# A bound on outstanding row gathers, and half of a projection in plain fp32

## The chip, the cores and the metric

The kernel runs on one core of a Trainium2 chip. The metric is the device time of one execution in microseconds (us). The core has five engines that run side by side and wait for each other through semaphores: PE (TensorE, matmuls; its weight loads are told apart as PEld), DVE (VectorE), ACT (ScalarE), POOL (GpSimd) and SP (SyncE, which here only issues DMAs). Each engine works off its own queue strictly in order.

## The reference

A decoder layer for one sequence of 256 tokens, model width 2048. First a mixer: one input projection to 4096 columns, whose first half feeds a gated linear recurrence (8 tiles of 128 channels) and whose second half feeds a gated causal convolution with 31 taps (8 tiles), and an output projection. Then a retrieval layer:

```python
proj = h @ w_in                                     # 256 x 2048 @ 2048 x 4096
lru_x, lru_g, conf_v, conf_g = jnp.split(proj, 4 parts of 1024)
...
z = causal_depthwise_conv(conf_v * sigmoid(conf_g), conf_dw_w, conf_dw_b)
y = jnp.concatenate([y_lru, silu(layer_norm(z))]) @ w_out
...
q = (h @ wq).reshape(t, 8 heads, 2, 128)
scores = einsum('thpd,hpnd->thpn', q, subkeys)      # 2 x 128 scores a head
...                                                 # top 16 of each half, top 16 of their sums
u = jnp.take(u_table, expert_idx, axis=0)           # 16384 x 2048, 128 rows a token
act = jnp.einsum('cd,chkd->chk', h, u)
v = jnp.take(v_table, expert_idx, axis=0)
out = jnp.einsum('chk,chkd->cd', gates * gelu(act), v)
```

## The kernel before

Activations lie transposed, 128 channels on the partitions and 256 tokens beside each other. A matrix in fp32 is split into a part h that PE takes in its faster fp32 form (fp32r in the rows) and a remainder l: ACT copies (line 94), DVE subtracts (line 95). A product is then three matmuls: h by h, h by l, l by h (lines 351, 352, 354 in `slab`).

**The projection** (about 40 to 345 us). Ten of the 32 column tiles are begun early (`begin`), while the modulation vectors are made; the other 22 go through `proj`, each as two slabs of 8 row blocks of 128. A slab takes a buffer of the ring `fring` for its loaded weights and one each of `Hring` and `Lring` for the split. `conf` and `lru` call `proj` and put their own work on DVE, the 31 taps of the convolution above all (line 422). `modstep` puts a piece of other modulation matrices (line 276) between slabs. A scheduler orders the instructions of each engine by priorities. When the last convolution is summed (line 426), `confln` normalises (lines 473 and 476), and the output projection follows.

**The score stage** (about 496 to 1235 us). For eight heads the queries are made, and then the scores of all 128 x 128 experts' first 1536 columns are multiplied densely, a row of 128 experts at a time (`upiece`, `piece`: lines 762, 765, 766, 768), in 304 pieces of weights (256 of `u`, 48 of `wq`). The remaining 512 columns of the 128 experts of each token are fetched: a unit is one expert rank of 128 tokens, a gather (line 704, an indirect DMA issued by POOL) brings 128 rows of 2 KB into a buffer, and a dot product on DVE (line 710) uses it. There are 256 units; a head's end makes 32 new ones. The order on DVE is written by hand: after each piece `fill` spends what time DVE has left over, on the top-k of the heads (`tops`) or on dot products. `gathers` issues gathers as long as there are a free buffer, a unit and credit of transfer time:

```python
while free and units and clock[2] > 0:
    g = free.pop(0)
...
elif dots and dots[0][3] + LAG <= clock[0]:
    clock[1] -= dot()
```

`clock[0]` counts pieces, and a dot product comes at least `LAG` = 3 pieces behind its gather. The buffers are 6 in the region R and 30 in S, where rows of the score matrix come to stand later (`lend`, `retire`). A gather into a buffer that has been used before waits for the dot product that read it.

Of the kernel before, what the change touches and what calls it, by code (L numbers as in the profile page):

```python
# [21 lines left out]
T = 256  # L22
D = 2048
KT = D // 128
# [9 lines left out]
HP = 120  # L34
# [4 lines left out]
DOTS = 3  # L39
SLACK = 0  # L40
UG = 2
BURST = 1
AHEAD = 10
RB = 8
# [42 lines left out]
def build(nc, tc, A, stop=None):  # L87
# [5 lines left out]
    def split(h, l, src, eng=None):  # L93
        nc.scalar.activation(h, src, AF.Copy)  # L94
        (eng or nc.vector).tensor_tensor(l, src, h, op=OP.subtract)  # L95
# [65 lines left out]
    class Ring:  # L161
# [4 lines left out]
        def __call__(self):  # L166
# [8 lines left out]
    hH = lambda k: hcol(0, k)  # L175
    hL = lambda k: hcol(1, k)
# [6 lines left out]
    fring = PF.ring(4, KT // 2, 128)  # L183
    Hring = Ring([PR.t(8, 128) for i in range(3)] + [sb.t(8, 128)])
    Lring = Ring([PR.t(8, 128) for i in range(2)] + [sb.t(8, 128) for i in range(2)])
    yH, yL = PR.t(KT, T), PR.t(KT, T)
    xT = PF.t(KT, T)
    xn = yT = PF.t(KT, T)
    zc = yT[:, CT:, :]

    spare = [[v[:, a:a + 4, :].rearrange("p a b -> p (a b)").rearrange("p (k c) -> p k c", c=128) for a in at]
             for v, at in ((yT, (4,)), (yH, (8, 12)), (yL, (8, 12)))]
    zrow = PF.t(512, dt=BF)[:1]
    nc.gpsimd.memset(zrow, 0.0)
    ar = Area(0, RKB)
# [13 lines left out]
    xpR = tr_(2, T + LK - 1)  # L209
    zR = tr_(3, T + CK - 1)  # L210
    mx = ar.t(T)

    psA = ExitStack()
    pp = psA.enter_context(pool("pp", NPP, space=PSUM))
# [49 lines left out]
    def modfull(m, new, misc, ring, st, n, dma, k0=0, k1=KT):  # L264


        ps = new()
        for a in range(0, D, n):
            for k in range(k0, k1):
                t = ring()  # L270
                with tc.high_priority(offset=HP):
                    dma.dma_start(t.rearrange("p (g c) -> p g c", g=4),
                                  wm[k * 128:(k + 1) * 128, m * D:m * D + D]
                                  .rearrange("p (g c) -> p g c", g=4)[:, :, a // 4:(a + n) // 4])
                for g in range(4):
                    nc.tensor.matmul(ps[32 * g:32 * g + 32, a // 4:(a + n) // 4], cs32[:, k, :],  # L276
                                     t[:, g * n // 4:(g + 1) * n // 4], start=k == k0, stop=k == k1 - 1,
                                     tile_position=(0, 32 * g))
                if k < k1 - 1 or a + n < D:
                    yield  # L280
        s = st()
        nc.scalar.activation(s, ps, AF.Copy)
        tp = misc()
        for q in range(4):
            nc.tensor.transpose(tp[:, 128 * q:128 * q + 128], s[:, 128 * q:128 * q + 128], ident)
        nc.vector.tensor_tensor(pick(modc[:, m, :]), tp.rearrange("p (q j r) -> p j q r", q=4, r=32)[:, :, :, 0],
                                pick(bmc[:, m * KT:m * KT + KT] if k0 == 0 else modc[:, m, :]), op=OP.add)
        yield
# [46 lines left out]
    def hchunk(j):  # L335
        sl = slice(4 * j, 4 * j + 4)
        nc.vector.scalar_tensor_tensor(a1[:, sl], modc[:, 1, sl], 1.0, col("g_pre_mix")[:, sl], op0=OP.add, op1=OP.mult)
        for k in range(4 * j, 4 * j + 4):
            nc.vector.tensor_scalar(xn[:, k, :], xn[:, k, :], a1[:, k:k + 1], modc[:, 0, k:k + 1], op0=OP.mult, op1=OP.add)
            split(hH(k), hL(k), xn[:, k, :])  # L340

    KH = KT // 2

    def slab(ps, src, k0, k1, rh, rl, first, last):
        n = k1 - k0
        w, h, l = (x()[:, :n, :] for x in (fring, Hring, Lring))
        with tc.high_priority(offset=HP):
            nc.sync.dma_start(w, src[:, k0:k1, :])
            split(h, l, w)
        for k in range(k0, k1):  # L350
            nc.tensor.matmul(ps, h[:, k - k0, :], rh(k), start=first and k == k0, stop=False)  # L351
            nc.tensor.matmul(ps, h[:, k - k0, :], rl(k), start=False, stop=False)  # L352
        for k in range(k0, k1):
            nc.tensor.matmul(ps, l[:, k - k0, :], rh(k), start=False, stop=last and k == k1 - 1)  # L354

    mring = lambda: wring().rearrange("p a b -> p (a b)")
    mods = itertools.chain(*(modfull(m, lambda: pp.tile([128, 512], F32, name="modps"), misc, mring, modsR, D, nc.sync)
                             for m in (2, 4, 3)))

    def modstep(n=1):  # L360
        for _ in range(n):
            next(mods, None)
# [14 lines left out]
    for j in range(4):  # L377
# [5 lines left out]
                        begin(j - 1, i)  # L383
                n += 1
        hchunk(j)
    rings = fring, Hring, Lring
    for r, more in zip(rings, spare):
        r.aps = r.aps + more
    for i in range(NFIRST):
# [5 lines left out]
    def proj(ct):  # L395
        if ct in begun:
            i = ct // CT % 2
            return begun.pop(ct)[:, (1 - i if ct >= 2 * CT else i) * T:][:, :T]
        ps = accum()
        for a in range(2):  # L400
            slab(ps, A["w_in"][ct], a * KH, a * KH + KH, hH, hL, a == 0, a == 1)
            modstep(next(mcount))
        return ps

    zs = yT[:, 0, :]
    lwa = PCOLS["lru_conv_w"][0]

    def conf(c):
        pg = proj(3 * CT + c)
        sg = sgR()  # L410
        nc.scalar.activation(sg, pg, AF.Tanh, scale=0.5)
        pv = proj(2 * CT + c)
        z = zR()
        nc.gpsimd.memset(z[:, :CK - 1], 0.0)
        nc.vector.scalar_tensor_tensor(z[:, CK - 1:], sg, 1.0, pv, op0=OP.add, op1=OP.mult)
        o = zc[:, c, :]
        for j in range(CK):
            wcol = wdw[:, j * CT + c:j * CT + c + 1]
            if j == 0:
                nc.vector.tensor_scalar(o, z[:, 0:T], wcol, col("conf_dw_b", c), op0=OP.mult, op1=OP.add)  # L420
            else:
                nc.vector.scalar_tensor_tensor(o, z[:, j:j + T], wcol, o, op0=OP.mult, op1=OP.add)  # L422
        if c == 1:
            nc.vector.tensor_tensor(zs, zc[:, 0, :], o, op=OP.add)
        elif c:
            nc.vector.tensor_tensor(zs, zs, o, op=OP.add)

    def lru(c):
        px = proj(c)
        lw = lwR().rearrange("p (a b) -> p a b", a=2)  # L430
        nc.sync.dma_start(lw, A["wax"][c])
# [71 lines left out]
    last = []  # L503
    GO = 4
    for g in range(0, KT, GO):
# [6 lines left out]
        for i in range(GO):  # L512
            k = g + i
# [5 lines left out]
            if k == KT - 1:  # L519
                last = to  # L520
# [85 lines left out]
    def flat(a, n):  # L606

        return Sf[:, a * T:(a + n) * T]
# [24 lines left out]
    units = []  # L633
# [62 lines left out]
    tops, free, dots, gone, lent, late = [], list(guS), [], [], {}, []  # L696
    clock = [0, 0.0, 0.0]

    def gathers():
        while free and units and clock[2] > 0:  # L700
            clock[2] -= GU * 512 / 360
            g = free.pop(0)
            tt, s_ = units.pop(0)
            nc.gpsimd.indirect_dma_start(out=g, out_offset=None, in_=A["ug"],  # L704
                                         in_offset=bass.IndirectOffsetOnAxis(ap=ei[:, tt, s_:s_ + 1], axis=0))
            dots.append((g, tt, s_, clock[0]))

    def dot():
        g, tt, s_, _ = dots.pop(0)
        nc.vector.scalar_tensor_tensor(gjR(), g, 1.0, h2n[:, tt, :GU], op0=OP.mult, op1=OP.mult,  # L710
                                       accum_out=actg[:, tt, s_:s_ + 1])
        if not any(g is x for x in gone):
            free.append(g)
        return dve(GU)

    def retire(r):
# [11 lines left out]
    def lend(at):  # L728
        lent[at] = flat(at, UG)[:, :GU]
        free.append(lent[at])  # L730

    def fill(ns, load, pe):

        clock[0] += 1
        clock[1] += ns
        clock[2] = min(clock[2] + (pe - load) * DMAF, BURST * GU * 512 / 360)
        gathers()
# [53 lines left out]

    for at in list(range(12, 60 - 3 * XUF - UG, UG)) + list(range(102, 129 - UG, UG)):
        lend(at)
    more = [flat(60 - 3 * i - 3, 3) for i in range(XUF)]
    with tc.manual_schedule(engines={mybir.EngineType.DVE}):
        for h in range(NH):
# [15 lines left out]
            for tt in range(2):  # L812
                ps = misc()
# [21 lines left out]
    last = xa.ring(int(xa.end - xa.at) // (UW * 128), UW * 128).aps  # L835
    with tc.manual_schedule(engines={mybir.EngineType.DVE}):
        while urows or state["parts"]:
            upiece()
        while dots or units:
            clock[2] = 1e9  # L840
            gathers()
            dot()
# [6 lines left out]
    for tt in range(2):  # L849
        ps = misc()  # L850
# [99 lines left out]
    for tt in range(2):  # L950
# [7 lines left out]
        ps = pm.tile([128, 512], F32, name="pm")  # L958
# [6 lines left out]
    ps = pm.tile([128, 512], F32, name="pm")  # L965
# [10 lines left out]
    units = [(tt, s_) for tt in range(2) for s_ in range(NK)]  # L976
# [34 lines left out]
    def vload(r, eng=None):  # L1011
        v, vh, vl = vfR(), vHr(), vLr()
        with tc.high_priority(offset=HPV):
            nc.sync.dma_start(v, A["vd"][r])
            split(vh, vl, v, eng)
        return vh, vl
# [17 lines left out]
    with tc.manual_schedule(engines=MANV):  # L1034
# [3 lines left out]
        for r in range(NK):  # L1038
            if r < 2:
                vmul(r, ws[r], vs[r], (1,))  # L1040
            else:
                v, w = vload(r), wnext
# [28 lines left out]
    with tc.manual_schedule(engines=MANV):  # L1071
        for tt in range(2):
# [10 lines left out]
            for n in (3, 0, 1, 2):  # L1083
                c = slice(512 * n, 512 * n + 512)
                src = out[tt][n] if c.stop <= DV else og[:, tt, :]
# [48 lines left out]
```

## Time and profile before

| what | value |
|---|---|
| runs | 2002.36 us median of 3 (2001.26 to 2014.05) |
| the profiled execution | 1990.23 us, its span 1988.5 us |
| busy share of the span | PE 92%, PEld 79%, DVE 77%, ACT 49%, POOL 34% |
| bytes moved by DMA | 530.07 MB, mean 267 GB/s |
| largest shares of the chain that ended last | PE 55%, issue 16%, POOL 11%, DMA 9%, DVE 5% |

The profile is of one execution. Times in its rows are counted from the start of the span. "Busy" is the time in which an engine had an instruction under way; matmuls overlap, so that one of them lasts longer than the time from its start to the next one's. The granted clock is 1.00 at PE's upper level (2.4 GHz) and 0.50 at its lower (1.2 GHz). "issue" as the end of a wait means that the profile names nothing that was waited for.

### The profile page before, as it was taken

To read this page: it belongs to the slowest core of one execution; us is meant where nothing else is said; L and a number is where in the kernel's file an instruction comes from. 1 tells how busy PE (TensorE), PEld (TensorE's weight loads), DVE (VectorE), ACT (ScalarE), POOL (GpSimd) and SP (SyncE) were. 2 spreads that over 40 slices of the span, in tenths; PEclk is the share of its full clock that TensorE was granted. 3 is DMA by queue.
4 is the path that set the end of the run, shared out by engine and by line. 5 is a ranking of instruction groups with operands and counts; after the bars stand their busy time and mean duration, and the time that the engine had idled before them with its cause. 6 is when DMAs were issued, how large, how long until landed. Compare 5 with 4: busy or idle time off the path is not lost.

```text
span 1988.5 us, 34804 instructions
## 1 busy us (share of the span) xinstructions
PE 1827.9 (92%) x12408; PEld 1580.1 (79%) x12408; DVE 1530.5 (77%) x3834; ACT 972.3 (49%) x1512; POOL 674.8 (34%) x577
## 2 busy tenths in 40 slices
PE   7897999898949699999899999999999999999996
PEld 3675787685949699999899999789877777778874
DVE  3249999755729489999787775789788888888887
ACT  3244434743625355555455555567544444544453
POOL 0000000000061432323543442224377666666662
PEclk8999999998979799999999999999999999999998
DMA  9988868686776677778898887742499898888884
GB/s 326 373 313 320 281 229 317 262 287 245 230 239 195 216 252 256 261 244 280 289 300 274 290 289 221 212 139 81 131 319 329 327 324 310 313 300 316 311 303 161
DMA packets 174799, 530.07 MB, mean 267 GB/s; under 512 B 20753, under 2 KB 44449, under 8 KB 167201
## 3 DMA queue, kind: packets, MB, share of 16 engines
q1 hardware_dynamic: 132656, 391.50, 57.8%
q0 software_dynamic: 40960, 134.25, 20.0%
q8 instruction: 97, 1.59, 0.3%
q10 hardware_dynamic: 1008, 2.10, 0.3%
q14 instruction: 78, 0.63, 0.1%
HBM read 521.40 MB, written 6.37 MB: 265 GB/s over the span
## 4 chain that ended last, share of the span: by engine, by line
PE 55%; issue 16%; POOL 11%; DMA 9%; DVE 5%; ACT 2%; another core or an unknown queue 1%; POOLq 0%; SPq 0%; ACTq 0%; DVEq 0%
PE acc L765 11%; PE acc L766 11%; PE acc L768 11%; POOL S L996 7%; PE acc L354 4%; PE acc L351 4%; PE acc L352 3%; PE W L945 3%; PE modps L276 3%; PE G L920 2%; DMA PF<-in_w_mod_dram 2%; POOL sl L996 2%; DMA PF<-in_w_in_dram 2%; POOL sh L996 2%; DVE PF L422 2%
## 5 line engine op out<-in xcount | busy, mean ns | idle before, releaser
L765 PE MATMUL acc<-sh,sb 128*128 128x256 f32 x1792 | 453.4, 288 | 36.8 <-issue 23.2
L766 PE MATMUL acc<-sl,sb 128*128 128x256 f32 x1792 | 452.1, 287 | 0.3 <-issue 0.3
L765 PEld LDWEIGHTS acc<-sh,sb 128*128 128x128 f32 x1792 | 349.3, 195 | 42.0 <-issue 25.1
L766 PEld LDWEIGHTS acc<-sl,sb 128*128 128x128 f32 x1792 | 349.3, 195 | 2.3 <-issue 2.2
L94 ACT ACTIVATE sb<-R 128x768 fp32r<-128x768 f32 (+2 forms) x203 | 196.8, 970 | 262.3 <-PE acc L766 115.2
L95 DVE TENSOR_TENSOR sb<-S,sb 128x768 fp32r<-128x768 f32 (+3 forms) x272 | 219.8, 809 | 130.7 <-ACT sb L94 106.1
L768 PE MATMUL acc<-sh,sb 128*128 128x256 f32 x1792 | 269.3, 285 | 9.9 <-issue 9.3
L94 ACT ACTIVATE sb<-S 128x768 fp32r<-128x768 f32 (+3 forms) x274 | 207.4, 759 | 140.0 <-PE acc L766 85.9
L996 POOL DMA_INDIRECT S<-in_vg_dram,ei x158 | 212.7, 1346 | 112.3 <-DVE R L1005 82.5
L768 PEld LDWEIGHTS acc<-sh,sb 128*128 128x128 f32 x1792 | 240.0, 194 | 10.1 <-issue 9.1
L704 POOL DMA_INDIRECT R<-in_ug_dram,ei x111 | 112.5, 1013 | 390.7 <-DMA R<-in_ud_dram 252.3
L95 DVE TENSOR_TENSOR sb<-R,sb 128x768 fp32r<-128x768 f32 (+1 forms) x160 | 150.2, 939 | 109.7 <-ACT sb L94 64.7
L704 POOL DMA_INDIRECT S<-in_ug_dram,ei x145 | 147.0, 1014 | 246.8 <-DVE R L710 156.3
L1023 PE MATMUL o<-sl,sb 128*128 128x512 f32 x900 | 221.4, 394 | 9.9 <-DVE sl L95 8.2
L1023 PE MATMUL o<-sh,sb 128*128 128x512 f32 x888 | 219.0, 395 | 10.1 <-DVE sh L95 9.3
L1023 PEld LDWEIGHTS o<-sl,sb 128*128 128x128 f32 x900 | 166.6, 188 | 53.8 <-DVE sl L95 17.9
L1023 PEld LDWEIGHTS o<-sh,sb 128*128 128x128 f32 x888 | 165.8, 189 | 53.9 <-DVE sh L95 18.2
L94 ACT ACTIVATE PR<-PF 128x1024 fp32r<-128x1024 f32 (+2 forms) x99 | 85.0, 868 | 127.5 <-DMA PF<-in_w_in_dram 85.5
L1023 PE MATMUL o<-sb 128*128 128x512 f32 x516 | 126.8, 391 | 1.5 <-ACT sb L94 1.5
L1005 DVE SCALAR_TENSOR_TENSOR R<-S,R 128x512 f32<-128x512 f32 x157 | 117.3, 747 | 3.5 <-DMA S<-in_vg_dram,ei 0.7
L351 PE MATMUL acc<-sh,PR 128*128 128x256 f32 x412 | 107.4, 296 | 8.8 <-ACT PR L94 7.1
L1023 PEld LDWEIGHTS o<-sb 128*128 128x128 f32 x516 | 96.6, 188 | 23.2 <-ACT sb L94 2.8
(304 smaller groups left out, 3436.3 us busy)
## 6 DMA issues: line engine op xcount, KB each, us to landing
R<-in_vd_dram SPq DMA_DIRECT2D x128, 768.0 KB
PF<-in_w_mod_dram SPq DMA_DIRECT2D x86, 1024.0 KB
R<-in_ud_dram SPq DMA_DIRECT2D x132, 384.0 KB
S<-in_ud_dram SPq DMA_DIRECT2D x124, 384.0 KB
PF<-in_w_in_dram SPq DMA_DIRECT2D x44, 512.0 KB
PF<-in_w_out_dram SPq DMA_DIRECT2D x32, 512.0 KB
PF<-in_w_in_dram SPq DMA_DIRECT2D x40, 256.0 KB
sl<-in_w_mod_dram SPq DMA_DIRECT2D x20, 512.0 KB
```

What stands on the lines that cost most here:

```text
L94: nc.scalar.activation(h, src, AF.Copy)
L95: (eng or nc.vector).tensor_tensor(l, src, h, op=OP.subtract)
L276: nc.tensor.matmul(ps[32 * g:32 * g + 32, a // 4:(a + n) // 4], cs32[:, k, :], t[:, g * n // 4:(g + 1) * n // 4], start=k == k0, stop=k == ...
L351: nc.tensor.matmul(ps, h[:, k - k0, :], rh(k), start=first and k == k0, stop=False)
L354: nc.tensor.matmul(ps, l[:, k - k0, :], rh(k), start=False, stop=last and k == k1 - 1)
L704: nc.gpsimd.indirect_dma_start(out=g, out_offset=None, in_=A["ug"], in_offset=bass.IndirectOffsetOnAxis(ap=ei[:, tt, s_:s_ + 1], axis=0))
L765: nc.tensor.matmul(ps, uh[:, k - k0, :], hH(k), start=k == 0, stop=False)
L766: nc.tensor.matmul(ps, uh[:, k - k0, :], hL(k), start=False, stop=False)
L768: nc.tensor.matmul(ps, ul[:, k - k0, :], hH(k), start=False, stop=k == end - 1)
L996: nc.gpsimd.indirect_dma_start(out=g, out_offset=None, in_=A["vg"], in_offset=bass.IndirectOffsetOnAxis(ap=ei[:, tt, s_:s_ + 1], axis=0))
L1005: nc.vector.scalar_tensor_tensor(og[:, tt, :], g, wn[:, tt, s_:s_ + 1], og[:, tt, :], op0=OP.mult, op1=OP.add)
L1023: nc.tensor.matmul(out[tt][n], a[:, tt * 128:tt * 128 + 128], b[:, 512 * n:512 * n + 512], start=r == 0 and a is wh and b is vh, stop=r == ...
```

## The change

Two parts. In the score stage the number of gathers whose dot product is still to come is bounded by 6, and from piece 60 on by one more for every 6 pieces; and a buffer that a dot product frees is put at the head of the free list, not at its end. In `proj` the first 8 row blocks of each of the 22 tiles are multiplied as they were loaded, by `slab32`: one fp32 matmul instead of three on split operands, with the unsplit activations `xn` as the moving operand. `xn` must therefore stay, so the buffer that `fring` had in addition there (five instead of four) is given up, and the sum `zs` gets a place of its own.

```diff
+OUT0 = 6
+OUTC = 60
+OUTS = 6
...
-             for v, at in ((yT, (4,)), (yH, (8, 12)), (yL, (8, 12)))]
+             for v, at in ((yH, (8, 12)), (yL, (8, 12)))]
...
+    zs = ar.t(T)
...
+    def slab32(ps, src, k0, k1, rhs, first, last):
+
+        w = fring()[:, :k1 - k0, :]
+        with tc.high_priority(offset=HP):
+            nc.sync.dma_start(w, src[:, k0:k1, :])
+        for k in range(k0, k1):
+            nc.tensor.matmul(ps, w[:, k - k0, :], rhs(k), start=first and k == k0, stop=last and k == k1 - 1)
...
-    rings = fring, Hring, Lring
+    rings = Hring, Lring
...
         for a in range(2):
-            slab(ps, A["w_in"][ct], a * KH, a * KH + KH, hH, hL, a == 0, a == 1)
+            if a:
+                slab(ps, A["w_in"][ct], KH, KT, hH, hL, False, True)
+            else:
+                slab32(ps, A["w_in"][ct], 0, KH, lambda k: xn[:, k, :], True, False)
             modstep(next(mcount))
...
-    zs = yT[:, 0, :]
...
+    def out_max():
+
+
+        return OUT0 + max(0, clock[0] - OUTC) // OUTS
+
     def gathers():
-        while free and units and clock[2] > 0:
+        while free and units and clock[2] > 0 and len(dots) < out_max():
...
         if not any(g is x for x in gone):
-            free.append(g)
+            free.insert(0, g)
```

On POOL, at the start of the score stage, before (`R` and `S` are the regions of the buffers; a row is a run of like instructions):

```order
L414 MEMSET R 128x30
L433 MEMSET R 128x3 x2
L704 DMA R<-in_ug_dram,ei 128x512 x6
L704 DMA S<-in_ug_dram,ei 128x512 x30
L704 DMA R<-in_ug_dram,ei 128x512 x6
L704 DMA S<-in_ug_dram,ei 128x512 x27
```

and after the change:

```order
L428 MEMSET R 128x30
L447 MEMSET R 128x3 x2
L723 DMA R<-in_ug_dram,ei 128x512 x18
L723 DMA S<-in_ug_dram,ei 128x512
L723 DMA R<-in_ug_dram,ei 128x512
L723 DMA S<-in_ug_dram,ei 128x512
L723 DMA R<-in_ug_dram,ei 128x512 x3
L723 DMA S<-in_ug_dram,ei 128x512
```

The gathers went round all 36 buffers; now the same six of R come again and again, and those of S come in one by one.

On DVE, near the end of the projection, before (`acc` is a finished projection tile, line 422 a tap of the convolution, line 95 of 128x1024 the split of one slab):

```order
L415 SCALAR_TENSOR_TENSOR R<-R,acc 128x256
L426 TENSOR_TENSOR PF<-PF 128x256
L420 TENSOR_SCALAR PF<-R 128x256
L95 TENSOR_TENSOR PR<-PF,PR 128x1024
L422 SCALAR_TENSOR_TENSOR PF<-R,PF 128x256
L95 TENSOR_TENSOR PR<-PF,PR 128x1024
L422 SCALAR_TENSOR_TENSOR PF<-R,PF 128x256
L95 TENSOR_TENSOR PR<-PF,PR 128x1024
L422 SCALAR_TENSOR_TENSOR PF<-R,PF 128x256
L439 TENSOR_SCALAR R<-R 128x256
```

and after (lines 429, 440, 434, 98, 436 and 453 are the former 415, 426, 420, 95, 422 and 439):

```order
L429 SCALAR_TENSOR_TENSOR R<-R,acc 128x256
L436 SCALAR_TENSOR_TENSOR PF<-R,PF 128x256
L434 TENSOR_SCALAR PF<-R 128x256
L436 SCALAR_TENSOR_TENSOR PF<-R,PF 128x256 x2
L440 TENSOR_TENSOR R<-R,PF 128x256
L436 SCALAR_TENSOR_TENSOR PF<-R,PF 128x256
L98 TENSOR_TENSOR PR<-PF,PR 128x1024
L436 SCALAR_TENSOR_TENSOR PF<-R,PF 128x256
L453 TENSOR_SCALAR R<-R 128x256
```

Of three splits between a tile's arrival and the recurrence's convolution (line 439, now 453) one is left.

## Rows read from the trace of the kernel before

**Rows 1.** Busy us and (x records) of each engine by stretch, score stage.

```profile
core 0: us, PE busy (x) PEld busy (x) DVE busy (x) ACT busy (x) POOL busy (x), PEclk, DMA share, GB/s
560.00:600.00 40.00, 12.03 (x62) 10.58 (x61) 3.25 (x9) 4.71 (x8) 25.21 (x27) 0.65 0.69 220
600.00:640.00 40.00, 40.00 (x325) 40.00 (x325) 38.81 (x168) 22.00 (x50) 4.33 (x4) 0.97 0.63 182
640.00:675.00 35.00, 15.96 (x94) 13.78 (x94) 8.70 (x20) 6.20 (x11) 23.91 (x24) 0.70 0.78 259
675.00:700.00 25.00, 25.00 (x200) 25.00 (x200) 23.95 (x106) 15.71 (x38) 3.77 (x3) 0.94 0.62 195
700.00:750.00 50.00, 47.53 (x393) 46.92 (x392) 44.16 (x179) 27.34 (x59) 18.36 (x19) 1.00 0.81 258
950.00:1000.00 50.00, 44.72 (x345) 43.77 (x344) 39.50 (x100) 23.63 (x36) 27.01 (x26) 0.93 0.87 289
1050.00:1100.00 50.00, 50.00 (x419) 50.00 (x418) 36.44 (x70) 26.18 (x35) 17.31 (x18) 1.00 0.86 271
```

**Rows 2.** The same view of line 704 alone: POOL busy (x gathers), clock, DMA.

```profile
552.00:593.00 41.00, 30.90 (x32) 0.74 0.80 251
634.00:671.00 37.00, 28.24 (x27) 0.77 0.82 265
709.00:720.00 11.00, 8.33 (x8) 1.00 0.91 298
```

**Rows 3.** Waits from 550 to 700 us: in total, times, longest.

```profile
DVE sb L95 <- issue: 51.0, 5, 32.9
PE acc L765 <- issue: 21.4, 3, 16.8
SPq L762 <- DVE R L643: 48.2, 2, 34.3
```

**Rows 4.** Timeline of DVE: start, duration, engine, line, operation.

```profile
559.28 0.68 DVE L710 SCALAR_TENSOR_TENSOR R<-R,h2n 128x512 bf16<-128x512 f32 x1
...
564.73 0.68 DVE L710 SCALAR_TENSOR_TENSOR R<-R,h2n 128x512 bf16<-128x512 f32 x1
...
598.31 0.96 DVE L95 TENSOR_TENSOR sb<-R,sb 128x768 fp32r<-128x768 f32 x1 [32.90 <-issue]
```

**Rows 5.** Timeline of SP's queue.

```profile
559.38 40.25 SPq L762 DMA_DIRECT2D R<-in_ud_dram  x3
```

**Rows 6.** Busy us by stretch, projection; columns as in rows 1.

```profile
150.00:200.00 50.00, 40.69 (x287) 30.35 (x288) 49.93 (x113) 20.41 (x29) 0.35 (x3) 0.93 0.84 322
200.00:250.00 50.00, 46.53 (x332) 37.45 (x331) 47.42 (x94) 22.12 (x30) 0.45 (x4) 0.93 0.81 275
250.00:300.00 50.00, 50.00 (x380) 41.84 (x379) 47.67 (x96) 20.57 (x27) 0.23 (x2) 1.00 0.67 237
300.00:350.00 50.00, 44.68 (x349) 34.57 (x347) 45.40 (x88) 20.82 (x28) 0.10 (x1) 1.00 0.87 317
```

**Rows 7.** Timeline of DVE at the projection's end.

```profile
352.08 0.42 DVE L426 TENSOR_TENSOR PF<-PF 128x256 f32<-128x256 f32 x1
...
365.39 2.76 DVE L476 TENSOR_TENSOR PF<-PF,R 128x256 f32<-128x256 f32 x8
```

**Rows 8.** Timeline of POOL: the first gather.

```profile
552.66 1.63 POOL L704 DMA_INDIRECT R<-in_ug_dram,ei  x1 [252.28 <-DMA R<-in_ud_dram]
```

**Rows 9.** Timeline of PE: fp32 matmuls; last, line 444's durations in ns.

```profile
13.99 1.13 PE L301 MATMUL misc<-R 128*128 128x256 f32 x4
...
176.76 0.70 PE L443 MATMUL misc<-R 128*128 128x256 f32 x2
177.30 0.59 PE L444 MATMUL misc<-R 128*128 128x256 f32 x2
...
L444 PE MATMUL misc<-R x16: 378/379/379, 151.0 to 362.5; 128*128 128x256 f32 x16
```

**Rows 10.** Timeline of DVE: one slab's split and the tap behind it.

```profile
295.11 1.22 DVE L95 TENSOR_TENSOR PR<-PF,PR 128x1024 fp32r<-128x1024 f32 x1
296.24 0.48 DVE L422 SCALAR_TENSOR_TENSOR PF<-R,PF 128x256 f32<-128x256 f32 x1
```

## The prediction

> **What bounds the kernel now.** I read the page's busy slices first, and then the table of stretches over the score stage (496 to 1235 us), because there the TensorE (PE) slice drops twice. In the stretches the reader is to see that PE is the bound of that stage: from 1050 to 1100 us it is busy all the time, with 419 matmul records in 50 us, while VectorE (DVE) has room [rows 1]. Against that, 560 to 600 us holds 62 records and 640 to 675 us holds 94, at a granted clock of 0.65 and 0.70 [rows 1]. So I looked for what else is special in these two stretches. The same stretches for the gathers alone show it: GpSimd (POOL) issues 32 row gathers between 552 and 593 us and 27 between 634 and 671 us, one every 1.25 us and without a pause, while a run of 8 from 709 to 720 us costs next to nothing (700 to 750 us still has 393 records) [rows 1, 2]. Then the waits and the timelines tell who stands still: DVE's longest wait, 32.9 us, ends with "issue", that is with nothing that the profile names, and so does PE's longest, 16.8 us [rows 3]. DVE ends a dot product at 565.4 us and starts its next instruction at 598.31 us [rows 4]. The queue of SyncE (SP) issues three weight loads in 40.25 us, waiting up to 34.3 us for DVE [rows 3, 5]. So the loads are not late because the bandwidth is gone. The engines' hand-offs are held while the burst lasts, and they come back when it ends.
>
> The second place is the projection, 150 to 350 us, where two engines are near full: DVE is busy 190.4 of 200 us (sum of the four stretches), PE 181.9 [rows 6]. It ends in a DVE chain: the last convolution's sum is at 352.08 us, the normalisation is over at 365.39 plus 2.76 us [rows 7], and the next stage's matmuls begin behind it.
>
> **The gathers: why the burst goes.** In the kernel before, the free list is first in, first out, and the order on POOL shows 6 buffers in R and 30 in S before the first is used again: the first 36 gathers wait for no dot product, only for their indices. One head's two halves give 32 units, which is the first burst. In the changed kernel the fifth gather already takes the buffer that the first dot product has freed, and among the first 18 none is outside the six buffers of R. POOL then stands in its queue behind DVE's dot products, which come about once in a piece of weights (18 matmuls, 2.16 us by 6 x 3 x 0.12 us). Nothing else is queued on POOL in this stage, so the wait itself costs nobody. The number of gathers and dot products stays 256, and by the bookkeeping of `fill` the last dot product falls at piece 294 of 304, as before, so no tail grows.
>
> The gain, from the two stretches: DVE-rich work runs at 325 records in 40 us [rows 1], that is 8.1 per us. The 62 records are 7.6 us of work in 40 us, so 32.4 us are lost; the 94 are 11.6 us in 35 us, 23.4 us lost. Together 55.8 us. After each stall the clock climbs from its lower level (0.97 and 0.94 over the next stretches [rows 1]), which is 0.03 x 40 + 0.06 x 25 = 2.7 us more. I take back 3 us for the first gathers of each head, which still come close together. From 950 to 1000 us there are 345 records instead of 419, 8.8 us; there DVE is itself busier, since dot products that were put off are caught up, and I count 3 us of it. Sum: 55.8 + 2.7 - 3 + 3 = **58 us less**. The bounds: 46 if each of the other six heads costs another 2 us, 67 if all of the 8.8 us and the 3 us come back.
>
> What could take this back is that a gather now leaves late. In the last 100 pieces three or four are under way, and a gather is issued behind the dot product of the piece before its own, four pieces ahead of its own dot product: 4 x 2.16 = 8.6 us. The first gather is issued at 552.66 us and its dot product runs at 559.28 us without having waited [rows 4, 8]: a gather lands in at most 6.6 us. So 2 us are left, and DVE's dot products should not wait. If they did, the splits of the weights that stand behind them on DVE would be late, and PE with them.
>
> **The projection: fp32 for half the rows.** 22 column tiles have 8 row blocks each, 176 in all, in which three matmuls on split operands give way to one in fp32. The split kind, of the same shape, passes at 419 in 50 us where nothing holds it [rows 1]: 0.12 us each, 0.36 for three. An fp32 matmul shows as two records; the two of one at 177.30 us take 0.59 us, of which the second's own 0.38 [rows 9], so they start 0.21 apart, 0.43 for the pair. Four elsewhere take 1.13 us, (1.13 - 0.38) / 3 = 0.25 apart, 0.50 a pair as the upper bound [rows 9]. PE gets 176 x (0.43 - 0.36) = 12.3 us more, between 11 and 25. DVE loses 22 subtractions of 128x1024, 1.13 us from one start to the next [rows 10]: 24.9 us less. ScalarE loses as many copies, which count for nothing: it is busy 20 of 50 us in this stage [rows 6]. The same bytes are loaded, but a buffer of the fp32 half is held until PE has read it and no longer until DVE has split it, and there are four instead of five. That leaves two tiles ahead, about 2 x 8 x (0.43 + 0.36) = 12.6 us for a load; what hides it is PE's own work, and where that cover is gone PE waits.
>
> Of 200 us PE is idle 18.1 and DVE 9.6 [rows 6]. With 12.3 us more work PE becomes the bound, and the stretch can shrink by at most 18.1 - 12.3 = 5.8 us. The chain at its end can begin earlier by the DVE work taken out there, some four splits of the last eight, 4.5 us. I take **4 us less**, from 14 less (both, with some idle time behind 350 us) to 12 more (none of PE's idle time comes back), and 25 more at fp32's upper price.
>
> **Sum.** Against the profiled execution's own 1990.23 us: 1990.2 - 58 - 4 = 1928. The median of the runs shown is 2002.36, 12 us above that execution, and I carry the difference over: 2002.4 - 62 = **1940 us**.
>
> **Rivals.**
> First, the bound doesn't cure the stall, because it hangs on something else that happens at a head's end (32 units at once, the indices, the tables of ScalarE), and not on POOL's run of gathers. For it: the profile names no cause for the waits. Against it: both stalls lie inside a long run and end with it, and from 700 to 750 us, where another head ends and the run is of 8, there are 393 records in 50 us [rows 1, 2]. Half of the 58 us at most would come: 2002 - 29 - 4 = 1969, and 1998 if none.
> By the Trainium skill (DMA: Bandwidth & Descriptors, section Queues, rings and completion order) an SDMA engine takes turns between its queues, a packet at a time, so the gathers could at most halve the rate of the weights. By that rule a burst is no reason for a standstill and bounding it gains little, which is this rival's 1998 us. The row of SP speaks against applying it here: the loads are not slow in the engines, they are not issued [rows 5].
>
> Second, the projection turns against it: none of PE's idle time comes back, and fp32 costs 0.50 us a pair, or the loads come late. Then 12 to 25 us more there, and 2002 - 58 + 12 = 1956 to 1969.
>
> Third, on the other side: fp32 records on changing weights are not overlapped but take their full 0.38 us [rows 9]. 352 x 0.38 = 134 us take the place of 528 x 0.12 = 63 us, PE is the bound in that stage, so + 70 us, and 2002 - 58 + 70 = 2014: slower. It decides from (58 + 63) / 352 = 0.34 us a record on. Against it: the pair at 177.30 us follows two records with another weight at 176.76, 0.54 us earlier [rows 9].
>
> **How the numbers follow.** The forecast, both parts within their bounds, gets 0.78 (1924 to 1956). The first rival has 0.10, the second 0.08, the third 0.03; 0.01 is for a greater gain. The range goes from 1920 to 1968, which takes in the second rival's lower half and leaves the first and third out. One per cent, 20 us, is about what a measurement of this kernel can tell from no change: faster 0.91, same 0.06, slower 0.03.
>
> **What would show it.** In the profile after: no stretch of 40 us with fewer than 300 records between 540 and 680 us; no run of more than about eight gathers 1.25 us apart, POOL waiting for DVE's dot products instead; the score stage some 58 us shorter, with dot products that don't wait for gathers. In the projection: fp32 pairs 0.43 us apart, DVE below 85% busy, PE without idle time, the last convolution's sum within 10 us of 352. I am wrong if PE stands still with "issue" waits although the gathers are spaced, or if DVE waits for a gather in the last 100 pieces.

## The result, and the profile after

The changed kernel takes 1943.26 us in the median of 4 runs (1936.9 to 1950.9), the kernel before 2003.6 beside it: a ratio of 0.969, 95% interval 0.964 to 0.974. The profiled execution took 1944.42 us, its span is 1942.7. The time is where the prediction put it. The way to it isn't.

| stretch of the span | before | after | difference | predicted |
|---|---|---|---|---|
| to the first matmul of the score stage | 496.4 | 476.0 | -20.4 | -4 |
| score stage, first to last record of lines 765 to 768 (now 784 to 787) | 737.6 | 702.2 | -35.4 | -58 |
| behind it | 754.5 | 764.5 | +10.0 | 0 |

In a second pair of profiles (E5 and E6 below) the three are -21.3, -28.0 and +1.7; the 10 us behind the stage don't come again, so I put them down to these two executions and not to the change.

Stretches of the score stage after the change, columns as in rows 1:

```profile
core 0: us, PE busy (x) PEld busy (x) DVE busy (x) ACT busy (x) POOL busy (x), PEclk, DMA share, GB/s
590.00:630.00 40.00, 31.03 (x240) 30.46 (x239) 26.05 (x93) 17.59 (x39) 16.98 (x18) 0.87 0.81 255
640.00:680.00 40.00, 34.38 (x268) 33.98 (x267) 29.35 (x114) 18.79 (x41) 16.01 (x17) 0.91 0.81 256
700.00:740.00 40.00, 29.86 (x225) 29.16 (x224) 24.73 (x91) 16.24 (x37) 17.99 (x19) 0.83 0.78 248
...
1050.00:1100.00 50.00, 50.00 (x419) 50.00 (x418) 36.31 (x70) 26.23 (x35) 23.28 (x24) 1.00 0.87 276
```

The two holes of 62 and 94 records [rows 1] are gone, but 240, 268 and 225 records in 40 us aren't the 325 of a stretch without stall. Several shallow ones stand in their place. Line 723, the gathers, in four of those places (POOL busy, gathers, clock, DMA), which answers to rows 2:

```profile
core 0: us, POOL busy (x), PEclk, DMA share, GB/s
533.00:543.00 10.00, 7.48 (x7) 1.00 0.85 282
586.00:603.00 17.00, 12.08 (x12) 0.84 0.92 309
645.00:666.00 21.00, 12.31 (x13) 0.84 0.82 261
702.00:716.00 14.00, 10.66 (x11) 0.79 0.94 332
```

and the waits from 530 to 730 us (in total, times, longest):

```profile
POOL R L723 <- DVE R L729: 74.1, 16, 8.2
...
DVE sb L98 <- issue: 22.6, 8, 6.9
...
PE misc L834 <- issue: 19.1, 5, 8.2
```

POOL now waits for the dot products, as was meant, and issues runs of 7 to 12 where it issued 32. Inside these runs PE and DVE still wait for nothing that the profile names, up to 8.2 us at a time instead of 16.8 and 32.9 [rows 3]. The dot products themselves waited for a gather's landing twice in 256 times, 0.6 us in all.

In the projection, busy time up to the score stage, first before, with cuts at the end of the last convolution's sum and at the first score matmul:

```profile
0.00:150.00 150.00, 125.07 (x837) 82.15 (x837) 56.57 (x141) 50.88 (x97) 1.33 (x13) 0.93 0.94 337
150.00:352.50 202.50, 181.90 (x1340) 144.20 (x1340) 192.82 (x394) 83.93 (x111) 1.13 (x10) 0.96 0.80 289
352.50:496.40 143.90, 133.34 (x990) 105.47 (x990) 90.46 (x157) 74.08 (x130) 0.00 (x0) 0.95 0.73 261
sum 496.40, PE 440.31 PEld 331.82 DVE 339.85 ACT 208.89 POOL 2.46; mean PE 146.77 PEld 110.61 DVE 113.28 ACT 69.63 POOL 0.82
```

and after:

```profile
0.00:150.00 150.00, 128.95 (x865) 83.79 (x865) 62.60 (x157) 52.72 (x101) 1.33 (x13) 0.94 0.97 348
150.00:323.70 173.70, 169.88 (x1056) 128.57 (x1052) 160.78 (x349) 59.81 (x81) 1.26 (x10) 1.00 0.86 299
323.70:476.00 152.30, 145.12 (x1074) 114.31 (x1074) 95.62 (x164) 76.89 (x135) 0.00 (x0) 0.96 0.76 277
sum 476.00, PE 443.96 PEld 326.67 DVE 319.00 ACT 189.41 POOL 2.59; mean PE 147.99 PEld 108.89 DVE 106.33 ACT 63.14 POOL 0.86
```

PE is busy 3.7 us more and idle 24.1 us less (56.1 before, 32.0 after); DVE has 20.9 us less to do. The stretch to the last sum shrinks by 28.8 us; 84 more of PE's records then lie behind it (1074 for 990), which gives 8 us back. DVE at the end of it (start, duration, line), which answers to rows 7:

```profile
323.31 0.42 DVE L440 TENSOR_TENSOR R<-R,PF 128x256 f32<-128x256 f32 x1
...
336.62 2.76 DVE L490 TENSOR_TENSOR PF<-PF,R 128x256 f32<-128x256 f32 x8
```

Eight of the new matmuls in a row show the price of an fp32 record:

```profile
213.09 1.99 PE L366 MATMUL acc<-PF 128*128 128x256 f32 x8
...
215.78 1.89 PE L366 MATMUL acc<-PF 128*128 128x256 f32 x8
```

(1.89 - 0.38) / 7 = 0.216 us from one to the next, 0.43 a pair; in the first row 0.23 and 0.46.

### The profile page after: what moved, and what is told of

Its sections match the earlier page's. It is cut to its first block, busy times and chain, and to the rows that moved or that the text cites. A ratio compares the mean times of both kernels' runs of the same rounds, so it can differ in the third digit from the quotient of the medians.

```text
span 1942.7 us, 34359 instructions
## 1 busy us (share of the span) xinstructions
PE 1828.0 (94%) x12232; PEld 1573.2 (81%) x12232; DVE 1511.7 (78%) x3812; ACT 952.7 (49%) x1491; POOL 672.7 (35%) x577
## 5 line engine op out<-in xcount | busy, mean ns | idle before, releaser
L723 POOL DMA_INDIRECT R<-in_ug_dram,ei x158 | 158.4, 1002 | 474.3 <-ACT ei L704 255.1
L723 POOL DMA_INDIRECT S<-in_ug_dram,ei x98 | 101.2, 1033 | 133.2 <-DVE R L729 106.0
L1042 PEld LDWEIGHTS o<-sb 128*128 128x128 f32 x516 | 97.7, 190 | 24.9 <-ACT sb L97 3.9
L97 ACT ACTIVATE PR<-PF 128x1024 fp32r<-128x1024 f32 (+2 forms) x81 | 66.3, 827 | 96.6 <-DMA PF<-in_w_in_dram 61.8
L97 ACT ACTIVATE sl<-R 128x1536 fp32r<-128x1536 f32 x43 | 64.1, 1492 | 96.1 <-DMA R<-in_vd_dram 90.6
```

The costliest lines, as they stand in the source:

```text
L1042: nc.tensor.matmul(out[tt][n], a[:, tt * 128:tt * 128 + 128], b[:, 512 * n:512 * n + 512], start=r == 0 and a is wh and b is vh, stop=r == ...
```

## The experiments

They ran on three chips. E1 to E4 ran on one where the kernel before takes 1915.01 us (14 runs), E9 to E12 on one where it takes 1917.56 (13 runs); I call these two quiet. E5 to E8 ran on a third, where it takes 2002.27 (7 runs), as where it was first measured. Ratios are to the kernel before on the same chip. "Stage" is the score stage, from the first to the last record of its dense matmuls. A "run" of gathers is a row of them whose starts on POOL lie at most 2.2 us apart; 1.25 us is the least. Each chip was met at one time only, so what I call a chip may also be its state at that time.

| | kernel | median us | ratio (95%) | last conv. sum | stage |
|---|---|---|---|---|---|
| E1 | gathers' part alone | 1919.22 | 1.001 (1.000 to 1.003) | 352.6 | 664.9 |
| E2 | projection's part alone | 1896.08 | 0.992 (0.989 to 0.994) | 322.0 | 660.6 |
| E3 | bound, freed buffer last | 1897.97 | 0.990 (0.987 to 0.993) | 327.5 | 661.9 |
| E4 | freed buffer first, no bound | 1895.03 | 0.990 (0.986 to 0.994) | 324.4 | 661.2 |
| E5 | before, again | 1994.27 (one) | | 353.4 | 735.9 |
| E6 | after, again | 1942.24 | 0.970 (0.967 to 0.974) | 325.0 | 707.9 |
| E7 | paced by score rows | 1959.94 | 0.981 (0.977 to 0.985) | 322.1 | 722.3 |
| E8 | bound of six to the end | 1917.76 | 0.959 (0.956 to 0.963) | 324.8 | 673.7 |
| E9 | bound of six to piece 140 | 1905.86 | 0.994 (0.992 to 0.996) | 323.9 | 665.2 |
| E10 | rows of 1 KB, no bound | 1896.29 | 0.990 (0.988 to 0.992) | 322.0 | 661.4 |
| E11 | fp32, split done all the same | 1923.12 | 1.004 (1.002 to 1.006) | 346.9 | 664.4 |
| E12 | both halves in fp32 | 1943.54 | 1.014 (1.011 to 1.017) | 350.3 | 664.0 |

**E1: the gathers' part alone.** The bound and the list's order in the kernel before.

> The bound and the last-freed-first list, with the projection as before. Theory from the two traces: the score stage gave 35 us and the projection 20, each by itself, so this kernel is 35 us below the kernel before (near 1967) with a score stage of about 702 us in place of 738. Rival, the sizes of the prediction: the gathers are worth 58 and the projection 4, the traces mix them up because a shift of the stage moves its stalls; then 1944.

Neither came. There was nothing to gain on this chip.

**E2: the projection's part alone.**

```diff
-        while free and units and clock[2] > 0 and len(dots) < out_max():
+        while free and units and clock[2] > 0:
...
-            free.insert(0, g)
+            free.append(g)
```

> The fp32 half and its ring, with the gathers as before. Theory: 20 us below the kernel before (near 1982), the last convolution's sum at about 324 us, and the score stage with its two long stalls, about 738 us long. Rival, the prediction's size: 4 us, near 1998.

The gain is the theory's, 18.9 us in the medians. But the stage with the gathers of before is 660.6 us long, not 738. Stretches of it and, of line 723 alone, the two runs of 32:

```profile
core 0: us, PE busy (x) PEld busy (x) DVE busy (x) ACT busy (x) POOL busy (x), PEclk, DMA share, GB/s
530.00:575.00 45.00, 44.92 (x375) 44.72 (x374) 38.84 (x159) 26.76 (x55) 35.70 (x31) 1.00 0.96 339
575.00:625.00 50.00, 50.00 (x416) 49.69 (x415) 46.75 (x182) 28.42 (x60) 36.60 (x33) 1.00 0.98 354
```

```profile
core 0: us, POOL busy (x), PEclk, DMA share, GB/s
529.00:576.00 47.00, 37.16 (x32) 1.00 0.96 337
577.00:622.00 45.00, 34.90 (x32) 1.00 0.98 353
```

64 gathers, 42 of the 63 steps between them 1.25 to 1.3 us and most others 1.5 to 2.0, and PE stands still for 0.08 us of 95. The first 32 take 45.8 us from start to start, in the kernel before on the first chip 39.5; whether this small difference in pace has a part in the stall wasn't tested. The DMA engines move 339 and 354 GB/s, gathers and weights side by side. A long run of gathers at this pace is therefore not enough for the stall. The second half of the theory, a stage of 738 us, was a miss.

**E3 and E4: one half of the gathers' part each.**

```diff
-            free.insert(0, g)
+            free.append(g)
```

> The changed kernel, but a freed buffer goes to the end of the list again; the bound stays. Theory: POOL is held by nothing but the dot product that last read the buffer it wants. With 36 buffers in turn the bound in the planner's books holds nothing on the chip: gathers in runs of about 30 as before, both long stalls, a score stage of about 738 us and a time near 1980. Rival: the order of dot products among top-k work, which the bound changes, is what cures the stall: near 1943.

E4 instead takes the bound away, `and len(dots) < out_max()`.

> The changed kernel without the bound; a freed buffer still goes to the head of the list. Theory: reuse ties POOL to the dot products, so most of the gain stays; the first run is some 10 to 12 gathers in place of 7, which costs 2 to 8 us more than the changed kernel: 1945 to 1952. Rival: the bound does the work: near 1980.

The times tell nothing of the halves, since this chip has no stall to cure. Of the expectations' times none came (1980 and 1943, 1945 to 1952 and 1980). What each half does to POOL is seen in the starts of line 723: with the bound alone, runs of 32, 28 and 38 gathers, as without it; with the list's order alone, at most 19. The bound stands in the planner's books, while on the chip a gather waits only for the dot product that last read its buffer.

**E5 and E6: both kernels again.**

> The kernel before, unchanged. The runs so far: its time was 2002 us where it was first measured and 1915 us beside the last four kernels, and a kernel with the same gathers (runs of 32, 32 and 36, one each 1.25 us) ran through them there without a stall. Theory: what delays the hand-offs between engines in a long run of gathers is a condition of the chip at that time, and not of the program; where the time is near 1915, the profile shows the same runs of 32 gathers, no stretch of 40 us between 540 and 700 us with fewer than 300 records of PE, and ScalarE's copies of the head's scores 0.2 us or less behind PE. Rival: the stall belongs to this program (its order of dot products, its addresses), and comes in its profile wherever it runs, also at 1915.

> The changed kernel, unchanged. Theory: where the kernel before takes about 1915 us, the bound is worth nothing and the fp32 half 19 us: ratio 0.990, near 1896. Where the kernel before takes about 2002, the ratio is 0.969 again. Rival: the two parts help each other (an earlier start of the score stage meets other transfers), and the ratio is 0.975 or below in either case.

This chip stalls, and the ratio is that of the first measurement. E6's case of a time near 2002 holds, but its rival, 0.975 or below, isn't told from it by 0.970: neither part was run alone on this chip. The case of a time near 1915, in both expectations, didn't arise: neither kernel was profiled on a quiet chip. That the stall belongs to the program alone is still ruled out, by the time of the kernel before: 1915.01 and 1917.56 us on two chips, 2002.27 on this one. The kernel before on this chip, stretches and then line 704:

```profile
560.00:600.00 40.00, 12.27 (x66) 11.15 (x64) 3.54 (x7) 3.72 (x6) 25.98 (x28) 0.67 0.72 225
640.00:675.00 35.00, 17.30 (x87) 15.64 (x86) 8.31 (x19) 6.08 (x10) 21.90 (x23) 0.63 0.72 230
```

```profile
553.00:595.00 42.00, 31.30 (x32) 0.75 0.80 251
```

A run of 32 gathers as in E2, here 39.8 us long. What differs is the time from one engine to the next. A head ends with two groups of score matmuls (line 815, now 834), each copied by ACT (line 820, now 839), and the second group waits for the first copy. PE and ACT in E5:

```profile
560.92 0.61 PE L815 MATMUL misc<-S 128*128 128x128 f32 x4
...
572.20 1.22 PE L815 MATMUL misc<-S 128*128 128x128 f32 x4 [10.20 <-issue]
...
596.60 0.58 PE L765 MATMUL acc<-sh,sb 128*128 128x256 f32 x1 [16.68 <-issue]
```

```profile
571.77 0.38 ACT L820 ACTIVATE R<-misc 128x256 f32<-128x256 f32 x1 [5.02 <-remote]
579.55 0.38 ACT L820 ACTIVATE R<-misc 128x256 f32<-128x256 f32 x1 [7.41 <-PE acc L766]
595.71 0.84 ACT L94 ACTIVATE sb<-R 128x768 fp32r<-128x768 f32 x1 [15.77 <-remote]
```

```profile
599.30 0.96 DVE L95 TENSOR_TENSOR sb<-R,sb 128x768 fp32r<-128x768 f32 x1 [31.56 <-issue]
```

and in E2, inside its first run:

```profile
536.86 0.61 PE L834 MATMUL misc<-S 128*128 128x128 f32 x4
...
538.02 0.71 PE L834 MATMUL misc<-S 128*128 128x128 f32 x4
```

```profile
537.52 0.45 ACT L839 ACTIVATE R<-misc 128x256 f32<-128x256 f32 x1
538.76 0.39 ACT L839 ACTIVATE R<-misc 128x256 f32<-128x256 f32 x1 [0.80 <-PE misc L834]
```

In E2 the first copy starts 0.05 us after the last matmul ends (537.47); in E5 it starts 10.2 us after (561.53), and for the last 5.0 us of them ACT had finished everything ahead of it in its queue.

The late side is PE's signal. The kept trace also holds the updates of the semaphores, which the views don't print. In E5 those that PE makes behind the matmuls that end (by the trace's estimate) from 560.4 to 579.9 us are on record 3.6 to 22.8 us after them, taken in their order, and ACT and DVE start within 0.1 us of the one they wait for (571.74 for the copy at 571.77, 595.68 for 595.71; DVE stands from 566.36 to 599.26 at a wait for PE, and the update is on record at 599.22). In E2's two runs it is at most 0.02 us. The other way nothing is late: ACT's copies end at 572.15 and 596.55, and PE goes on at 572.20 and 596.60. So these waits do have a releaser. PE's two end with "issue" because ACT's updates of 572.15 and 596.55 are missing from the trace. A late load of instructions didn't end them: from 575 to 608 us, in which ACT, PE and DVE go on, the trace has packets of two queues only, gathers (q0) and weights (q1).

```profile
q0 software_dynamic: 1367, 4.46, 46.7%
q1 hardware_dynamic: 445, 1.22, 13.0%
```

One thing more sets the chips apart. Where the kernels stall, the trace lacks updates, in E5 nine in ten of DVE's missing ones in the score stage from the first gather on: 2685 of DVE's 2856 are on record in E5, and 17406 of the DMAs' 20496; in E2 all 2835 and 20491. It is so in all six traces with a stall (17406 to 17810) and in none of the eight without (20488 or more). Recording is thus disturbed together with the signals. Every run here has a recorded span and clock, so nothing shows whether the stall is there in an execution that isn't recorded.

**E7: spacing without the bound.** POOL reads a column of the last score row but one before the first gather of each row.

```diff
+            if state.get("tie") is not None:
+                nc.gpsimd.tensor_scalar(pz, state.pop("tie")[:, :1], ipart, None, op0=OP.is_equal)
             g = free.pop(0)
```

> The projection as changed; gathers without the bound and with freed buffers at the end of the list, but before the first gather of each row of scores POOL reads one column of the score row before it, so that it can't run ahead of PE. Up to 23 gathers are outstanding, in runs of 2 to 7. Theory: where hand-offs are slow, spacing does what the bound does, and 5 to 15 us more than it; where the kernel before takes 1915, it is worth nothing and costs at most 5: 1893 to 1901. Rival: the number of outstanding gathers matters and not their spacing; then it keeps the stalls where there are any.

It stalls more than the changed kernel, not less. Stretches of E7, then line 727, its gathers:

```profile
540.00:570.00 30.00, 17.67 (x104) 16.16 (x103) 11.06 (x45) 7.17 (x14) 20.28 (x24) 0.67 0.76 250
600.00:650.00 50.00, 37.53 (x254) 35.39 (x254) 26.92 (x90) 16.79 (x39) 30.14 (x32) 0.86 0.79 255
```

```profile
531.00:562.00 31.00, 23.31 (x23) 0.81 0.83 274
602.00:624.00 22.00, 16.64 (x16) 0.92 0.85 278
```

The pacing failed to space them. The likely reason, which wasn't tested, is that a head's indices come after the rows that POOL was to wait for, and then nothing holds it. So the theory's gain of 5 to 15 us didn't come, and E7 doesn't tell spacing from the number outstanding. It does give another point: runs of 23 and 16, and a stage between the others.

**E8: six to the end.**

```diff
-OUTS = 6
+OUTS = 1000
```

> The changed kernel with a bound that stays at 6 to the end, so that all 256 gathers go through the six buffers of R; by the planner's books seven dot products are left for the time after the last piece. Theory: where the kernel before takes 1915, no gain in the stage and a tail of 3 to 8 us: 1899 to 1904. Where hand-offs are slow, the runs of 7 to 12 gathers become shorter and 10 to 20 us come back, less the tail. Rival: the tail is hidden behind the last pieces on PE, and the time is that of the changed kernel.

The theory's gain and more, 24.5 us in the medians against E6. Two of its stretches, then line 723 at a head's end:

```profile
600.00:650.00 50.00, 50.00 (x416) 49.68 (x415) 45.63 (x183) 27.34 (x58) 19.19 (x20) 1.00 0.84 278
650.00:700.00 50.00, 48.40 (x399) 47.79 (x399) 44.36 (x182) 28.25 (x60) 18.27 (x18) 1.00 0.81 269
```

```profile
640.00:650.00 10.00, 6.52 (x7) 1.00 0.95 332
```

No run up to 800 us is longer than seven. The stage is 34.2 us shorter than in E6, within 13 of the quiet chips. The tail isn't hidden: PE's last score matmuls are at 1150.5 us, and the next stage's (line 939) begin at 1161.5, 10 us after those end, against 0.8 in E6 and 3 to 8 expected.

**E9: the bound kept to piece 140, then loosened by one for every 4 pieces.**

```diff
-OUTC = 60
-OUTS = 6
+OUTC = 140
+OUTS = 4
```

> The changed kernel with the bound of 6 kept until piece 140, and from there one more for every 4 pieces, so that by the planner's books the last dot product falls at piece 303 of 304 and none is left for the end. Theory: where the kernel before takes about 2000, the stage is as short as with six to the end (674 us), without the 10 us behind it: 1905 to 1912. Where it takes 1915, the same as the changed kernel within 4 us, near 1896. Rival: the stalls come back with the looser bound behind piece 140 (800 us and later): 1920 to 1935 on a chip that stalls.

On this quiet chip it has no tail (0.8 us from the stage to the next), and a stage of 665.2. It is 10 us above what was expected (1896), 4.6 of it in the stage (660.6 in E2). What it does on a chip that stalls was not measured.

**E10: half the bytes.**

```diff
-            nc.gpsimd.indirect_dma_start(out=g, out_offset=None, in_=A["ug"],
+            nc.gpsimd.indirect_dma_start(out=g[:, :GU // 2], out_offset=None, in_=A["ug"].rearrange("n (a b) -> (n a) b", a=2),
...
```

> The projection as changed, the gathers unbounded and freed buffers last, as in the kernel before; each gather brings 128 rows of 1 KB in place of 2 KB (from half the index's place in the table), and the dot products multiply 256 columns instead of 512, so half of the remaining columns is left out. The same 256 gathers, 1.25 us each on POOL. Theory, for a chip on which the kernel before takes about 2000: hand-offs wait for POOL's unbroken issue of gathers, not for their bytes; long runs keep their stalls and the stage takes 710 to 735 us. Rival: the bytes do it (gathers at 210 GB/s beside 180 of weights); with half of them the stage falls to 660 to 690. Where the kernel before takes 1915 it says nothing: about 661 us of stage.

A quiet chip again, so it says nothing of the stall, as expected for that case. 661.4 us against 660.6 with full rows in E2: where nothing stalls, the gathers' bytes are hidden.

**E11: fp32, but the split is done.** In `slab32`, behind the load:

```diff
+            split(Hring()[:, :k1 - k0, :], Lring()[:, :k1 - k0, :], w)
```

> The changed kernel, but the first half of each of the 22 tiles is still split by ScalarE and DVE, with nobody reading the result, while PE multiplies it in fp32. DVE and ScalarE have the work of before, PE that of after. Theory: what the projection gains is DVE's relief, so the last convolution's sum goes back from 324 to 350 us or later, and the kernel is 20 to 30 us slower than the changed one (near 1967 where the kernel before takes 2002, 1920 where it takes 1915). Rival: the gain comes from matmuls that no longer wait for a split (a shorter chain from load to PE); then the sum stays below 332 and the time within 8 us of the changed kernel.

The theory holds. Busy time up to the score stage:

```profile
150.00:346.90 196.90, 185.34 (x1136) 139.23 (x1134) 187.33 (x380) 79.83 (x104) 1.12 (x10) 0.97 0.79 283
...
sum 495.20, PE 449.61 PEld 331.48 DVE 340.11 ACT 208.66 POOL 2.45; mean PE 149.87 PEld 110.49 DVE 113.37 ACT 69.55 POOL 0.82
```

DVE has its 340 us again, and the score stage begins at 495.2 us, as before the change (496.4), though PE multiplies in fp32. ACT has its copies again too, but is busy 79.83 of the 196.9 us, DVE 187.33.

**E12: both halves in fp32.** The second half's activations share their place with the convolution's sums, which the program writes meanwhile; so these matmuls multiply what lies there, and wait for it.

```diff
-                slab(ps, A["w_in"][ct], KH, KT, hH, hL, False, True)
+                slab32(ps, A["w_in"][ct], KH, KT, lambda k: xn[:, k, :], False, True)
```

> The changed kernel with both halves of the 22 tiles in fp32. Theory: after the change PE is without idle time in the projection (3.9 us of 174), and a pair in fp32 takes 0.44 us where three split matmuls take 0.39, so 176 more of them cost 9 us, and DVE's further relief buys nothing: the last convolution's sum near 333 us, the kernel 5 to 12 us slower than the changed one. Rival: DVE, with the convolution's taps at the end, still sets the stage: 10 us faster.

Neither: 350.3 us, 26.6 us later than in the changed kernel. The waits from 150 to 350 us give most of the reason:

```profile
PEld acc L366 <- DVE PF L436: 22.0, 9, 5.5
```

PE's weight loads wait for taps of the convolution (line 436), which comes of this shared place and not of the price of fp32. The experiment doesn't tell whether PE or DVE bounds the projection after the change.

## Why the time was right and the steps weren't

**The gathers.** The reading was right on a chip that stalls: both stalls lie in long runs of gathers, hand-offs between engines are late there (10.2 us in E5, on PE's side), and fewer gathers at a time make the stage shorter, 735.9, 722.3, 707.9 and 673.7 us for longest runs (up to 800 us) of 32, 23, 14 and 7 in E5, E7, E6 and E8. E6 and E8 differ in the bound alone. The step that failed is "The engines' hand-offs are held while the burst lasts", told as what a burst does to this program. E2 has bursts as long and no late hand-off. The stall takes a second condition, which lies in the chip or in what happens around it, the recording included, and which nothing here shows. On the two quiet chips the bound is worth nothing; the four kernels there with bound and reordered list have stages of 664.0 to 665.2 us, the four without one of the two 660.6 to 661.9, so it costs some 3 us of stage.

The second failure is a size: "I take back 3 us". After the change 702.2 - 661 = 41 us of stall were left on a chip that stalls, not 3, because from piece 60 on the bound rises, and at the heads' ends near 590 and 705 us 12 and 11 gathers go in a row again (14 and 14 in E6). E8, where only that rise is taken out, has 13 us left. The forecast of no run above eight and of no 40 us with fewer than 300 records between 540 and 680 us fell with it; E8 comes near to what that forecast described, with runs of seven and, from 544 us on, 300 records or more in any 40 us. That dot products wouldn't wait was right, 0.6 us in all, and so was POOL's wait behind them, though it is the seventh gather and not the fifth that takes the first freed buffer (the sixth leaves at 540.36 us, the first dot product runs from 540.55, the seventh leaves at 541.76).

**The projection.** The step that failed is "PE becomes the bound, and the stretch can shrink by at most 18.1 - 12.3 = 5.8 us". Its prices were right: a pair at 0.43 us, DVE 20.9 us less (24.9 predicted). But it added PE's 12.3 us as if PE ran at its upper clock before as well. Up to the score stage PE's busy time rose by 3.7 us only: in the stretch to the last sum the granted clock was 0.96 before and is 1.00 now, which is worth some 8 us (an estimate, 0.04 x 202.5). And it looked for idle time from 150 to 350 us alone: 24.1 us went up to the score stage, 16.8 of them in the stretch to the last sum (20.6 before, 3.8 after). So of the 14.6 us between 5.8 and 20.4, 8.6 are PE's busy time and 6.0 its idle time. E11 shows that it is the splits' doing: with them back the score stage begins at 495.2. DVE's chain, the splits and taps in one queue, is what set this stage before, for ACT, which has the other half of a split, is busy 41% in E11 and DVE 95%; DVE's 20.9 us less go with the 20.4 gained. DVE is now busy 92.6% of the stretch to the last sum (160.78 of 173.7 us), not below 85%, since the stretch shrank with its work; PE is nearly without idle time there (3.8 us), as predicted. The last sum, forecast within 10 us of 352, came at 323.3.

**The sum.** -58 and -4 became about -41 and -19: in the medians on the stalling chip 60.0 us (2002.27 - 1942.24) came, and 18.9 of it is the projection, if it is worth there what E2 gained on a quiet one (the score stage begins 20.4 and 21.3 us earlier in the two pairs of profiles). By the profiles the stage gave 35.4 and 28.0. Two errors with opposite signs cancelled, some 15 us by the medians and more by the profiles: that the time came out right is luck. The 12 us between the profiled execution and the median, carried over, did no harm. And the bounds as named add up to 1921 to 1968 us, not to the 1924 to 1956 that got 0.78. On a quiet chip only the second part is left: E2 to E4 stand at 0.990 to 0.992 there. The changed kernel itself wasn't run on one.

**The rivals.** The first, that the bound doesn't cure the stall because it hangs on something else, was half right, and not as it was put: something else is needed, but it isn't the head's end, which comes eight times on every chip. With it stood the rule of the Trainium skill (DMA: Bandwidth & Descriptors, section Queues, rings and completion order) that an engine takes turns between its queues. E2 fits the rule, 337 to 353 GB/s over runs of 32 with PE fed. On the stalling chip such runs show 251 GB/s with PE starved, and the rule doesn't say why. The second rival (projection slower) and the third (fp32 records at 0.38 us) are out by the first table.

**What stays open.** What makes PE's signals late on one chip and not on two others, and whether they are late without a recording; whether POOL's unbroken issue, the bytes or the number outstanding feeds it there, since E7 didn't space the gathers and E10 met a quiet chip. Of the versions, E8 is the fastest where it stalls (0.959), E2 to E4 where it doesn't; E9 may be the best of both, but was measured on a quiet chip alone.

## What to carry to other kernels

A stall whose waits end with nothing that the profile names may belong to the chip, or to the recording, and not to the program: before it is priced, look at the same kernel's time on another chip, for here 75 us of a stage of 736 were gone there, and look whether the trace is whole, for here it lacked updates just where it stalled. A bound in a planner's books holds an engine only where a buffer's reuse turns it into a wait; look for the instruction that carries it. And where two engines are both near full, count the work taken from the one that the end hangs on, over the whole way to the next stage, before setting a limit by the other's idle time.

## What the runs showed of the hardware

ACT's copy behind PE's score matmuls starts 0.05 us after them on one chip and up to 10.2 us after them on another, in the same place of the program and under a run of 32 gathers. PE's semaphore updates are on record up to 22.8 us late there, ACT's copies reach PE within 0.05 us. Where nothing stalls, gathers and weight loads together moved 354 GB/s over 50 us with PE busy all the time. A matmul 128x128 by 128x256 in fp32 shows as two records, 0.216 us apart at the upper clock (granted 1.00 in that stretch).
